# Decays of two heads at a time in a hybrid decoder layer: which PSUM banks they use and where they stand in the program

## The chip, the cores and the metric

The kernel runs on one core of one Trainium2 chip. The metric is the device time of one execution in microseconds (us): lower is better.

## What is computed

The reference is one decoder layer over 512 tokens of width 1024, in fp32: a SwiGLU feed-forward, two parallel token mixers (a gated delta rule of 8 heads, and a convolution module of width 31), a cross-attention into 256 memory tokens, and a second SwiGLU feed-forward, with a LayerNorm after each. The change touches one quantity of the delta rule, the decay of a head:

```python
gc = jnp.cumsum(g.reshape(b, n, CHUNK, h).transpose(0, 3, 1, 2), axis=-1)
diff = gc[..., :, None] - gc[..., None, :]
decay = jnp.where(tri, jnp.exp(jnp.where(tri, diff, 0.0)), 0.0)
m = jnp.where(strict, jnp.einsum("bhncd,bhnmd->bhncm", kb, kc) * decay, 0.0)
...
a_qk = jnp.einsum("bhncd,bhnmd->bhncm", qc, kc) * decay
```

So a head's decay is a matrix of exponentials per chunk that does not depend on q, k or v. It multiplies two products of the head: k with k (`m`) and q with k (`a_qk`). The kernel works with chunks of 128 tokens, four to a head.

## The kernel before

**Stages.** The program runs the first feed-forward, then the mixers, the cross-attention and the second feed-forward. All large products are done in three passes (`wh*xh`, `wl*xh`, `wh*xl`), each weight tile being split into a high and a low part: ScalarE casts the high part (L362) and VectorE subtracts (L110). One output tile of 128 channels by 512 tokens (`tile_job`, `a_tile`) is 24 products into one of four `acc` banks. `Weights.next` makes the tile in use and two more ahead of it; the high parts have four buffers (`WB = 4`).

**Mixers.** `mixers` first makes the tiles of the convolution's input gate (`glu`, a Sigmoid), five pairs of tiles, m = 0 to 4. Behind them come ten stages p = 0 to 9. Stage p < 8 makes the k, q and v tiles of head p; stages 0 and 1 also make the last three pairs of the gate (two in stage 0, so stage 0 has seven tiles: k, lin, gate, lin, gate, q, v). From stage 2 on a z tile is added. When a tile is finished, a chain of small steps for the head starts: `head_k` (short convolution on ScalarE and VectorE, Silu, transposes, norms, the product k with k, then the multiplication with the decay), an inversion (`invert_blocks` on GpSimd, `invert_rest` on TensorE), the scan over the chunks (`scan`), `head_q` (transposes, the product q with k, the decay) and `head_v`.

**What sets the order.** Within the stages TensorE's instructions are issued in the order in which the program writes them. An `Agenda` counts time by the columns that TensorE has been given (512 columns count 512/2400 us). Each step of a chain says after how many of these microseconds the next one is due (`PACE`), and between the k-steps of a tile (three products) the agenda runs every step that is due. So a step's TensorE instructions stand at a fixed place among the products of the tiles. If their operands are late, everything behind them on TensorE waits. Ahead of the stages there is no agenda. The order on ScalarE and VectorE is drawn up when the program is built, and each engine then takes its instructions in that order. Of the 31-tap convolution, VectorE gets a share between the steps (`taps`).

**PSUM.** There are four `acc` banks and four for the chains: `prep` has two, `inv` one, `scan` one (`BANKS`). `prep` is shared by the transposes of k, kb, q and v, the two products with the decay, and the decays; `inv` serves `invert_rest` and `scan` serves the scan, which also uses `acc` banks.

**A decay.** `decay` (L744) scales a triangle by the head's log-decays on ScalarE: eight instructions of 128x128 that make `ug` in two parts (`ug0`, `ug1`, one buffer each). Then it yields; in the agenda it goes on 6 us later. TensorE then makes three products of 128x512 into a `prep` bank, and ScalarE takes the exponential of the bank (L760) into `dd`. Heads 0 and 1 are done in the loop over m (at m = 3 and m = 4), heads 2 to 7 each at the start of the stage before their own (`if 2 <= p + 1 < HEADS`, L1177). Stage p's first microseconds are also when the q and v chains of head p - 1 come due. So TensorE takes the decay products of head p + 1 close to `head_v`'s transposes for head p - 1 (into the other `prep` bank) and to its product q with k, which needs a `prep` bank too.

ScalarE's Exp, Silu and Sigmoid each need another activation table: the rows call the switch ACT_TABLE_LOAD. Copy and Square are used between them without one.

Of the kernel before, what the change touches and what calls it, by code (L numbers as in the profile page):

```python
# [8 lines left out]
F32 = mybir.dt.float32  # L9
# [7 lines left out]
P = 128  # L17
# [17 lines left out]

TAPS = (5, 0.53, 4)
LAG = 3
PACE = dict(d=(6,), k=(6.6, 1.6, 4.6, 2.8), i=(37.5, 2, 3, 2, 2.3, 2, 2.5), b=(7.8, 1.25), s=(3.2, 2.1, 2.2, 1.8, 2.4, 2.1, 2.2, 1.5, 1.5, 3), q=(8, 5.5), v=(7.2,))
SLIP = 0
PAIRS = (2, 1)  # L40
GLU = 8 - sum(PAIRS)
# [257 lines left out]
class Kern:  # L299
# [441 lines left out]
        for j, t in enumerate((self.eg, self.edec, self.egl)):  # L741
            nc.scalar.activation(t.rearrange("p c h -> p (c h)"), cs[:, j * 32:(j + 1) * 32], AF.Exp)

    def decay(self, mp, h, dds):  # L744

        nc = self.nc
        ugs = []
        for i, g in enumerate((self.gh, self.gl)):
            ug = mp.tile([P, SEQ], F32R, name=self.nm("ug"), tag=f"ug{i}", bufs=1)
            for c in range(NCHK):  # L750
                nc.scalar.activation(ug[:, c * P:(c + 1) * P], self.con[:, K_U:K_U + P], AF.Copy,
                                     scale=g[:, c, h:h + 1].bitcast(F32))
            ugs.append(ug)
        yield
        ps = self.psum("prep")
        for i, ug in enumerate(ugs):
            self.mm(ps, lhsT=self.later, rhs=ug, start=(i == 0), stop=False)
        self.mm(ps, lhsT=self.idr, rhs=bc(self.never.unsqueeze(1), [P, NCHK, P]), start=False, stop=True)
        dd = mp.tile([P, SEQ], F32, name=self.nm("dd"), tag="dd", bufs=9)
        nc.scalar.activation(dd, ps, AF.Exp)  # L760
        dds[h] = dd

    def conv4(self, ps, dst, mt):

# [322 lines left out]
    def mixers(self, res, dst):  # L1087
        nc, tc = self.nc, self.tc
        S = 512
        with self.pages("mix") as (mp, self.small), ExitStack() as ctx:  # L1090
            ctx.enter_context(self.psum_pool("psm", **BANKS))
            self.small.tile([P, 8], F32, name="pad")
            cs, dds, self.convs, self.due = [], {}, [], 0

            def glu(pl, pg):
                m = len(cs)
                cs.append(self.glu(mp, m, pl, pg))
                self.convs.append(self.conv31(mp, m, cs[m]))
            ps = self.first
            for m in range(2):  # L1100
                glu(ps[2 * m], ps[2 * m + 1])
            self.gating(mp, self.a_tile())
            for m in range(2, GLU):
                lin = self.a_tile()
                self.taps(TAPS[0])
                glu(lin, self.a_tile())
                self.taps(TAPS[0])
                if m >= GLU - 2:
                    for _ in self.decay(mp, m - GLU + 2, dds):
                        pass  # L1110
            ozs = []
            with self.pages("heads") as (hp, self.small2):
                bufs = dict(kT=2, qT=3, ktok=3, MT=3, AT=3, vb=3, X=3, Y=3, tmp=4, z=3, bm=2, t1=2)

                def page(tag, dt=F32):
                    return hp.tile([P, S], dt, name=self.nm("pg"), tag=tag, bufs=bufs[tag])
                early = ["ktok", "X", "MT", "AT"] * 2
                late = ["bm", "t1", "ktok", "X", "MT", "AT", "bm", "t1"]
                hi_tags = ["kT"] * 2 + ["qT"] * 3 + ["z"] * 3
                lo_tags = ["vb"] * 3 + ["Y"] * 3 + ["tmp"] * 2  # L1120

                def pages(srcs):
                    hi, lo = [], []
                    for s, th, tl in zip(srcs, hi_tags, lo_tags):
                        hi.append(page(th, F32R))
                        lo.append(page(tl, F32R))
                        self.split(hi[-1], lo[-1], s)
                    return hi, lo

                def gate(tag):  # L1130
                    sg = page(tag)
                    nc.scalar.activation(sg, self.a_tile(), AF.Sigmoid)
                    return sg
                yp = []

                def tile_job(done):

                    ps = self.acc()
                    for k in self.a_steps(ps, self.W.next(), self.x_hi, self.x_lo, 0, SEQ):
                        if k == KT - 1:  # L1140
                            done(ps)
                        yield

                def gate_done(tag):
                    def done(ps):
                        yp.append(page(tag))
                        nc.scalar.activation(yp[-1], ps, AF.Sigmoid)
                    return done
                sts = [{} for _ in range(HEADS)]

                def on_k(h):
                    def chain(ps):
                        yield from paced(self.head_k(hp, h, ps, dds[h], sts[h]), PACE["k"])
                        yield from paced(self.invert_rest(hp, sts[h]), PACE["i"])
                        yield from paced(self.scan(mp, hp, h, sts[h], ozs), PACE["s"])
                    return lambda ps: agenda.start(chain(ps))

                def on_q(h):
                    return lambda ps: agenda.start(paced(self.head_q(hp, h, ps, sts[h]), PACE["q"]))

                def on_v(h):
                    return lambda ps: agenda.start(paced(self.head_v(hp, h, ps, sts[h]), PACE["v"]))
                self.bms = [page("bm"), page("bm")]
                for t in self.bms:
                    nc.gpsimd.memset(t, 0.0)
                self.agenda = agenda = Agenda()
                for p in range(HEADS + 2):
                    if p < HEADS:
                        jobs = [on_k(p), on_q(p), on_v(p)]
                    else:  # L1170
                        jobs = [gate_done(t) for t in early[4 * (p - HEADS):4 * (p - HEADS) + 4]]
                    for _ in range(PAIRS[p] if p < len(PAIRS) else 0):
                        lin = []
                        jobs[1:1] = [lin.append, lambda ps, lin=lin: glu(lin[0], ps)]
                    if p >= 2:
                        jobs.insert(0, lambda ps, p=p: self.head_z(hp, p - 2, ps, sts[p - 2]))
                    if 2 <= p + 1 < HEADS:  # L1177
                        agenda.start(paced(self.decay(mp, p + 1, dds), PACE["d"]))
                    for done in jobs:
                        for _ in tile_job(done):  # L1180
                            agenda.step()
                            self.taps(TAPS[1])
                agenda.finish()
                self.agenda = None
                oh, ol = pages(ozs)
                for m in range(8):
                    self.taps(TAPS[2])
                    ya = self.a_tile(lambda k, a, b: oh[k][:, a:b], lambda k, a, b: ol[k][:, a:b])
                    nc.vector.tensor_tensor(yp[m], yp[m], ya, op=ALU.mult)
                self.taps(8 * CW)  # L1190
                assert not self.convs
                sgc = []
                for t in range(NT):
                    for i, _ in enumerate(self.conv_norm(mp, cs, t)):
                        sgc.append(gate(late[2 * t]))
                    sgc.append(gate(late[2 * t + 1]))
                ch, cl = pages([c[:, 0:S] for c in cs])
                yh, yl = [], []
                for m in range(8):
                    yc = self.a_tile(lambda k, a, b: ch[k][:, a:b], lambda k, a, b: cl[k][:, a:b])  # L1200
                    nc.vector.scalar_tensor_tensor(sgc[m], yc, self.pcol(C_BCO + m), sgc[m], op0=ALU.add, op1=ALU.mult)
                    nc.vector.tensor_tensor(yp[m], yp[m], sgc[m], op=ALU.add)
                    h = mp.tile([P, S], F32R, name=self.nm("yh"), tag="dd", bufs=9)
                    l = mp.tile([P, S], F32R, name=self.nm("yl"), tag="c", bufs=8)
                    self.split(h, l, yp[m])
                    yh.append(h)
                    yl.append(l)
            ctx.close()
            with self.psum_pool("psl", gp=4), self.pages("ln2") as (lp, small):
                ln = LayerNorm(self, lp, small, 2, res, ALPHA, LN_EPS, dst, True)  # L1210
                self.b_form(KT, lambda k: yh[k], lambda k: yl[k], ln)
                self.first = ln.rest()
# [231 lines left out]
```

## Time and profile before

| what | value |
|---|---|
| median of 3 runs | 1533.62 us (1533.11 to 1535.7) |
| profiled execution, its own time | 1534.12 us |
| its span, first to last instruction | 1532.3 us |
| mean granted TensorE clock | 0.995 |
| TensorE busy | 1499.4 us, 98% of the span |
| VectorE, ScalarE, GpSimd busy | 961.4, 661.1, 156.9 us |

The span is that of the one profiled execution; 1.8 us of its own time lie outside the span. PE stands for TensorE's matmuls, PEld for its weight loads, DVE for VectorE, ACT for ScalarE, POOL for GpSimd. `L760` is line 760 of the kernel. A row such as `dd<-prep` is an instruction that reads tile `prep` and writes tile `dd`.

### The profile page before, as it was taken

How to read it: one execution, taken by the hardware profiler on the slowest of the kernel's cores; microseconds unless marked ns; L12 is line 12 of the kernel's file. 1: busy time of each engine (PE TensorE's matmuls, PEld its weight loads, DVE VectorE, ACT ScalarE, POOL GpSimd, SP SyncE). 2: the span in 40 equal slices, each digit the busy share in tenths (PEclk: the TensorE clock that was granted, in tenths of full speed). 3: DMA queues.
4: the chain of work that ended last, by engine and by line, in shares of the span. 5: the costliest groups of instructions: out<-in, count | busy, mean ns of one | idle time of the engine just before them, and what ended most of it. 6: DMA issues, size and time to landing. Idle time of an engine off the chain costs nothing.

```text
span 1532.3 us, 21736 instructions
## 1 busy us (share of the span) xinstructions
PE 1499.4 (98%) x8626; PEld 1296.3 (85%) x8626; DVE 961.4 (63%) x1356; ACT 661.1 (43%) x1236; POOL 156.9 (10%) x306
## 2 busy tenths in 40 slices
PE   7899999999999999999999999999999999999998
PEld 6899998889888777878888888899889888888886
DVE  7888875338879788778878355665756333333235
ACT  5455454232456766665553473134523222222110
POOL 0000000001004344444400000000000000000001
PEclk9999999999999999999999999999999999999999
DMA  7433325234132212222222223474324322222221
GB/s 274 177 111 111 111 70 178 97 110 165 56 102 90 90 61 70 78 79 78 89 101 83 83 74 118 167 255 149 119 85 163 138 97 96 96 97 96 96 97 55
DMA packets 65526, 170.97 MB, mean 112 GB/s; under 512 B 18768, under 2 KB 20944, under 8 KB 65360
## 3 DMA queue, kind: packets, MB, share of 16 engines
q1 hardware_dynamic: 65424, 169.57, 33.1%
q8 instruction: 68, 1.11, 0.3%
q14 instruction: 34, 0.28, 0.1%
HBM read 158.54 MB, written 12.06 MB: 111 GB/s over the span
## 4 chain that ended last, share of the span: by engine, by line
PE 83%; DVE 7%; issue 3%; POOL 3%; ACT 2%; DMA 2%; SPq 0%; DVEq 0%; POOLq 0%; ACTq 0%
PE acc L375 42%; PE acc L468 7%; PE gp L468 6%; PE acc L427 4%; PE acc L426 4%; PE acc L428 4%; PE gp L427 4%; PE gp L428 4%; PE gp L426 4%; PE inv L375 1%; DVE a L1042 1%; DVE wl L110 1%; POOL xt L778 1%; POOL xb L778 1%; DVE qT L110 1%
## 5 line engine op out<-in xcount | busy, mean ns | idle before, releaser
L110 DVE TENSOR_TENSOR wl<-w,wh 128x1024 fp32r<-128x1024 f32 (+1 forms) x220 | 265.3, 1209 | 309.5 <-ACT wh L362 308.4
L375 PE MATMUL acc<-xh,wh 128*128 128x512 f32 (+1 forms) x1032 | 396.7, 385 | 0.0
L375 PE MATMUL acc<-xl,wh 128*128 128x512 f32 (+1 forms) x1032 | 382.5, 371 | 0.1
L375 PE MATMUL acc<-xh,wl 128*128 128x512 f32 (+1 forms) x1032 | 382.0, 370 | 0.0
L362 ACT CAST wh<-w 128x1024 fp32r<-128x1024 f32 (+1 forms) x220 | 227.5, 1038 | 352.2 <-PE acc L375 135.4
L375 PEld LDWEIGHTS acc<-xl,wh 128*128 128x128 f32 x1032 | 194.4, 189 | 34.8 <-DVE xl L110 0.5
L375 PEld LDWEIGHTS acc<-xh,wh 128*128 128x128 f32 x1032 | 195.2, 189 | 28.7
L375 PEld LDWEIGHTS acc<-xh,wl 128*128 128x128 f32 x1032 | 195.4, 189 | 27.7
L1042 DVE SCALAR_TENSOR_TENSOR a<-c,par,a 128x512 f32<-128x512 f32 x232 | 174.8, 754 | 3.5
L261 POOL TENSOR_TENSOR mv<-mv,par 128x1 f32<-128x1 f32 x16 | 15.5, 971 | 986.0 <-DVE mv L260 986.0
L375 PE MATMUL acc<-pg,wh 128*128 128x512 f32 x256 | 79.8, 391 | 0.1
L375 PEld LDWEIGHTS acc<-pg,wh 128*128 128x128 f32 x256 | 48.0, 188 | 10.5 <-ACT pg L362 0.5
L468 PE MATMUL acc<-th,qh 128*128 128x256 f32 x176 | 50.9, 289 | 3.7 <-ACT qh L362 3.7
L468 PE MATMUL acc<-th,ql 128*128 128x256 f32 x176 | 51.0, 290 | 3.2 <-DVE ql L110 3.2
L682 DVE TENSOR_TENSOR s<-s,acc 128x512 f32<-128x512 f32 x22 | 15.1, 688 | 57.3 <-PE acc L375 57.2
L468 PE MATMUL acc<-tl,qh 128*128 128x256 f32 x176 | 50.6, 287 | 0.0
L375 PE MATMUL acc<-pg,wl 128*128 128x512 f32 x128 | 49.8, 391 | 0.0
L468 PE MATMUL gp<-th,qh 128*128 128x256 f32 x176 | 49.8, 283 | 0.0
L468 PE MATMUL gp<-th,ql 128*128 128x256 f32 x176 | 49.8, 283 | 0.0
L468 PE MATMUL gp<-tl,qh 128*128 128x256 f32 x176 | 49.8, 283 | 0.0
L681 ACT ACTIVATE s<-acc 128x512 f32<-128x512 f32 x22 | 13.1, 597 | 82.0 <-PE acc L375 82.0
L778 POOL TENSOR_TENSOR xb<-xb,xt 32x14 f32<-32x14 f32 (+6 forms) x112 | 47.5, 424 | 8.8
(377 smaller groups left out, 3135.8 us busy)
## 6 DMA issues: line engine op xcount, KB each, us to landing
w<-wall SPq DMA_DIRECT2D x216, 512.0 KB
res<-row SPq DMA_DIRECT2D x24, 256.0 KB
row<-res SPq DMA_DIRECT2D x12, 512.0 KB
wd<-wall SPq DMA_DIRECT2D x11, 512.0 KB
wc<-wall SPq DMA_DIRECT2D x11, 512.0 KB
wa<-wall SPq DMA_DIRECT2D x11, 512.0 KB
wb<-wall SPq DMA_DIRECT2D x11, 512.0 KB
lngb<-ln SPq DMA_DIRECT2D x8, 512.0 KB
```

The lines of the kernel that those rows point to most:

```text
L110: ins = getattr(self.kn.nc.vector, op)(*args, **kw)
L261: nc.gpsimd.tensor_tensor(mv[:, 3:4], mv[:, 2:3], self.kn.mh[:, 0:1], op=ALU.pow)
L362: self.nc.scalar.copy(hi, src)
L375: self.pin(self.nc.tensor.matmul(out, **kw), out.shape[-1] * (1 if kw["lhsT"].dtype == F32R else 4))
L426: mm(ps, lhsT=th, rhs=wh, start=first, stop=False)
L427: mm(ps, lhsT=th, rhs=wl, start=False, stop=False)
L428: mm(ps, lhsT=tl, rhs=wh, start=False, stop=last)
L468: self.tc.keep_in_program_order(self.nc.tensor.matmul(o, lhsT=a, rhs=b, start=(first and g == k == n == 0), stop=False, skip_group_check=T ...
L681: nc.scalar.activation(s, g, AF.Silu)
L682: nc.vector.tensor_tensor(s, s, u, op=ALU.mult)
L778: self.pool_pin(self.nc.gpsimd.tensor_tensor(out, x, y, op=op))
L1042: yield V.scalar_tensor_tensor(a, c[:, j:j + SEQ], w(j), a, op0=ALU.mult, op1=ALU.add)
```

## The change

`decay` becomes `decays` and takes two heads. For each of the two in turn it makes `ug`, yields, and issues the three products, the first head into the `inv` bank and the second into the `scan` bank. Behind both it issues the two exponentials one after the other. The pairs (0, 1) and (2, 3) are done in the loop over m, at m = 3 and m = 4; the pairs (4, 5) and (6, 7) are started in stage 0, at its first and at its fourth tile, with 6 us of agenda time ahead of each head's products. In the later stages there are no decays.

```diff
-PACE = dict(d=(6,), k=(6.6, 1.6, 4.6, 2.8), ...
+PACE = dict(d=(6, 6), k=(6.6, 1.6, 4.6, 2.8), ...
...
-    def decay(self, mp, h, dds):
+    def decays(self, mp, hs, dds):
 
         nc = self.nc
-        ugs = []
-        for i, g in enumerate((self.gh, self.gl)):
-            ug = mp.tile([P, SEQ], F32R, name=self.nm("ug"), tag=f"ug{i}", bufs=1)
-            for c in range(NCHK):
-                nc.scalar.activation(ug[:, c * P:(c + 1) * P], self.con[:, K_U:K_U + P], AF.Copy,
-                                     scale=g[:, c, h:h + 1].bitcast(F32))
-            ugs.append(ug)
-        yield
-        ps = self.psum("prep")
-        for i, ug in enumerate(ugs):
-            self.mm(ps, lhsT=self.later, rhs=ug, start=(i == 0), stop=False)
-        self.mm(ps, lhsT=self.idr, rhs=bc(self.never.unsqueeze(1), [P, NCHK, P]), start=False, stop=True)
-        dd = mp.tile([P, SEQ], F32, name=self.nm("dd"), tag="dd", bufs=9)
-        nc.scalar.activation(dd, ps, AF.Exp)
-        dds[h] = dd
+        banks = []
+        for h, tag in zip(hs, ("inv", "scan")):
+            ugs = []
+            for i, g in enumerate((self.gh, self.gl)):
+                ug = mp.tile([P, SEQ], F32R, name=self.nm("ug"), tag=f"ug{i}", bufs=1)
+                for c in range(NCHK):
+                    nc.scalar.activation(ug[:, c * P:(c + 1) * P], self.con[:, K_U:K_U + P], AF.Copy,
+                                         scale=g[:, c, h:h + 1].bitcast(F32))
+                ugs.append(ug)
+            yield
+            ps = self.psum(tag)
+            for i, ug in enumerate(ugs):
+                self.mm(ps, lhsT=self.later, rhs=ug, start=(i == 0), stop=False)
+            self.mm(ps, lhsT=self.idr, rhs=bc(self.never.unsqueeze(1), [P, NCHK, P]), start=False, stop=True)
+            banks.append(ps)
+        for h, ps in zip(hs, banks):
+            dds[h] = mp.tile([P, SEQ], F32, name=self.nm("dd"), tag="dd", bufs=9)
+            nc.scalar.activation(dds[h], ps, AF.Exp)
...
                 if m >= GLU - 2:
-                    for _ in self.decay(mp, m - GLU + 2, dds):
+                    for _ in self.decays(mp, (2 * (m - GLU + 2), 2 * (m - GLU + 2) + 1), dds):
                         pass
...
-                    if 2 <= p + 1 < HEADS:
-                        agenda.start(paced(self.decay(mp, p + 1, dds), PACE["d"]))
-                    for done in jobs:
+                    for i, done in enumerate(jobs):
+                        if p == 0 and i in (0, 3):
+                            hs = (4, 5) if i == 0 else (6, 7)
+                            agenda.start(paced(self.decays(mp, hs, dds), PACE["d"]))
                         for _ in tile_job(done):
                             agenda.step()
                             self.taps(TAPS[1])
```

## Rows read from the trace of the kernel before

**Rows 1.** The page: TensorE's busy time, and the chain that ended last.

```profile
PE 1499.4 (98%) x8626; PEld 1296.3 (85%) x8626; DVE 961.4 (63%) x1356; ACT 661.1 (43%) x1236; POOL 156.9 (10%) x306
...
PE 83%; DVE 7%; issue 3%; POOL 3%; ACT 2%; DMA 2%; SPq 0%; DVEq 0%; POOLq 0%; ACTq 0%
```

**Rows 2.** TensorE's waits from 400 to 800 us: total us, times, longest us.

```profile
PE prep L375 <- ACT dd L760: 5.4, 4, 2.3
PE prep L380 <- DVE AT L110: 0.8, 1, 0.8
PE prep L375 <- ACT vb L793: 0.7, 1, 0.7
```

**Rows 3.** Timeline, one of these waits, in stage 4: start, duration, instruction.

```profile
584.85 0.62 PE L375 MATMUL prep<-ug,later 128*128 128x512 f32 x2
...
585.54 0.60 PE L380 MATMUL prep<-con,vT 128*128 128x128 f32 x4
...
586.48 1.28 ACT L760 ACT_TABLE_LOAD   x1
587.78 0.60 ACT L760 ACTIVATE dd<-prep 128x512 f32<-128x512 f32 x1
...
588.43 1.75 PE L375 MATMUL prep<-qT,kT 128*128 128x128 f32 x8 [2.29 <-ACT dd L760]
```

**Rows 4.** Busy time by stretch around that wait; PEclk is the granted clock.

```profile
core 0: us, PE busy (x) PEld busy (x) DVE busy (x) ACT busy (x) POOL busy (x), PEclk, DMA share, GB/s
...
585.00:590.00 5.00, 2.71 (x17) 2.30 (x16) 2.35 (x4) 4.93 (x15) 0.00 (x0) 0.88 0.52 158
590.00:595.00 5.00, 5.00 (x24) 4.26 (x24) 2.12 (x4) 3.83 (x7) 2.02 (x2) 0.78 0.03 3
```

**Rows 5.** Busy time by stretch: stage 0 in two halves, then stages 1 to 6.

```profile
430.00:450.00 20.00, 20.00 (x92) 16.55 (x91) 14.86 (x23) 12.85 (x27) 2.19 (x4) 1.00 0.24 79
450.00:470.00 20.00, 20.00 (x96) 16.71 (x95) 19.54 (x25) 7.74 (x13) 5.39 (x11) 1.00 0.33 96
480.00:685.00 205.00, 196.24 (x1267) 161.67 (x1265) 163.61 (x258) 137.45 (x380) 82.50 (x166) 0.99 0.27 82
```

**Rows 6.** Timeline of TensorE in stage 7, which has no decay.

```profile
701.18 0.60 PE L380 MATMUL prep<-con,vT 128*128 128x128 f32 x4
701.62 1.06 PE L375 MATMUL prep<-qT,kT 128*128 128x128 f32 x8
```

**Rows 7.** Groups of ScalarE, 400 to 800 us: count, busy us, mean ns, idle before.

```profile
L751 ACT ACTIVATE ug<-con,gh 128x128 fp32r<-128x128 f32 x32 | 10.8, 402 | 0.0
L760 ACT ACT_TABLE_LOAD x8 | 10.3, 1283 | 0.1
...
L771 ACT ACT_TABLE_LOAD x5 | 6.4, 1283 | 8.3 <-DVE kT L110 4.5 <-DVE qT L110 3.8
L975 ACT ACT_TABLE_LOAD x5 | 6.4, 1283 | 0.1
```

**Rows 8.** Timeline of ScalarE around the start of stage 0.

```profile
421.98 1.27 ACT L751 ACTIVATE ug<-con,gh 128x128 fp32r<-128x128 f32 x4
423.16 1.27 ACT L751 ACTIVATE ug<-con,gl 128x128 fp32r<-128x128 f32 x4
...
432.60 1.04 ACT L362 CAST wh<-w 128x1024 fp32r<-128x1024 f32 x1
...
442.55 0.64 ACT L771 ACTIVATE kT<-kT 128x512 f32<-128x512 f32 x1
```

**Rows 9.** Timeline of TensorE around the start of stage 0.

```profile
430.44 0.39 PE L375 MATMUL prep<-never,idr 128*128 128x512 f32 x1
430.67 0.39 PE L375 MATMUL acc<-xh,wh 128*128 128x512 f32 x1
...
443.60 0.60 PE L380 MATMUL prep<-con,kT 128*128 128x128 f32 x4
```

More of the change, by code (lines that the diff above doesn't have):

```diff
@@ L37 @@
 LAG = 3
-PACE = dict(d=(6,), k=(6.6, 1.6, 4.6, 2.8), i=(37.5, 2, 3, 2, 2.3, 2, 2.5), b=(7.8, 1.25), s=(3.2, 2.1, 2.2, 1.8, 2.4, 2.1, 2.2, 1.5, 1.5, 3), q=(8, 5.5), v=(7.2,))
+PACE = dict(d=(6, 6), k=(6.6, 1.6, 4.6, 2.8), i=(37.5, 2, 3, 2, 2.3, 2, 2.5), b=(7.8, 1.25), s=(3.2, 2.1, 2.2, 1.8, 2.4, 2.1, 2.2, 1.5, 1.5, 3), q=(8, 5.5), v=(7.2,))
 SLIP = 0
```

## The prediction

> **What bounds the kernel now.** I read the page first. TensorE is busy for 98% of the span and carries 83% of the chain that ended last [rows 1]. So ScalarE time that the change saves is worth nothing by itself; only what TensorE waits for, and what its clock loses, can move the end. The change alters the stretch from 400 to 800 us, so I next asked for TensorE's waits there. The largest three are all for a `prep` bank that another engine still reads: 5.4 us in four waits for the decay's exponential, 0.8 us for `AT`, 0.7 us for `vb` [rows 2]. From 480 to 685 us, the stages with a decay, TensorE is idle for 205.00 - 196.24 = 8.8 us [rows 5]; 6.9 of them are these six waits.
>
> The timeline shows how one comes about [rows 3]. The decay's products start at 584.85 in one `prep` bank and the v transposes at 585.54 in the other. The product q with k is next and needs a bank. The exponential that frees the first bank stands behind an ACT_TABLE_LOAD of 1.28 us on ScalarE, starts at 587.78 and takes 0.60. TensorE goes on at 588.43, after 2.29 us. Then the granted clock is below full: 0.88 and 0.78 of it as means over two stretches of 5 us [rows 4], that is part of each at the lower level, 1.2 GHz. What TensorE did before was to stand idle for those 2.29 us.
>
> The trace holds its own control. At stage 7 there is no decay, and the same pair of instructions, v transposes at 701.18 and product q with k at 701.62, follows without a wait [rows 6].
>
> **The change part by part: the banks.** With `inv` and `scan` for the decays, and none in stages 1 to 6, the product q with k takes the `prep` bank that was freed before the v transposes, as in rows 6. The `AT` and `vb` waits have the same cause: a decay between two users of `prep` leaves them one bank to alternate in. So all six go. Their worth is at least the 6.9 us of idle time [rows 2]. It is a little more: a product is shown as 0.39 us long, while the next one starts 0.23 us after it (430.44 to 430.67 [rows 9]), so each wait hides another 0.16 us: 6.9 + 6 x 0.16 = 7.9 us. The upper bound is all idle time of the stretch, 8.8 us [rows 5]. I take 7.9. `inv` and `scan` are free at that time: their first users belong to head 0's inversion, which the agenda puts 37.5 us after `head_k`.
>
> **The clock.** (1 - 0.88) x 5 + (1 - 0.78) x 5 = 0.6 + 1.1 = 1.7 us of full-speed work [rows 4] come back, if no new wait of that length takes its place.
>
> **The exponentials side by side.** The eight loads in front of the decay's exponential become four; of the loads that restore Silu behind them (L771 and L975, five each [rows 7]) about six go with the decays of stages 1 to 6. That is ten times 1.28 us, 12.8 us of ScalarE. TensorE's chain does not hold them outside the waits already counted: no gain of their own. They can shorten the rest of the idle time, 8.8 - 6.9 = 1.9 us, or reordering can lengthen it; I take 0 with 1.9 either way.
>
> The Trainium skill, page "ScalarE: Activation LUTs", section "What ACT_TABLE_LOAD costs", puts a switch at about 1283 ns for the load and 1380 ns for a drain, 2.66 us in all. Rows 3 show the load at 1.28 us and the exponential 1.30 us after the load's start, so no drain of that length stands in the queue. By the Trainium skill's figure the four remaining pairs would each hold ScalarE 1.38 us longer; on the two loads near the critical place below that would be an estimated 2.8 us more of waiting and a sum of about 1528.8 us.
>
> **What is moved ahead.** The 24 decay products are all still made: nothing saved or added on TensorE. The `dd` tiles, nine buffers for eight decays and the outputs `oz`, suffice as before. No DMA is issued or moved. Weight casts run at least two tiles ahead of use; a tile is 24 products of 0.23, so they have 10.9 us, and ScalarE would have to be late by more than 9 before a tile waits for one.
>
> What can wait is a product with a fixed place. Scalings for one head take 424.43 - 421.98 = 2.45 us [rows 8], and `ug` has one buffer, so the next head's can begin only after the second product of the head before. At the start of stage 0 this becomes a chain. Head 2's products stand where head 1's did, until 430.7 [rows 9]. Head 3's scalings: to 433.1. Its products, three of 0.23: to 433.8. Load and two exponentials, 1.28 + 0.6 + 0.6: to 436.3. Head 4's scalings: to 438.8, or 439.8 with a cast of 1.04 [rows 8] between. Head 4's products are due 6 us of agenda after 430.67. The steps run every three products, so that is ten steps of 0.68, plus head 3's 0.7: 438.2. The wait is 0.6 to 1.6 us, and none where ScalarE takes the scalings ahead of the exponentials. Behind head 4's products in TensorE's queue stand the tiles of stage 0 and the transposes of head 0's k (443.60 [rows 9]), whose Silu ended at 442.55 + 0.64 = 443.19 [rows 8], only 0.4 us ahead; scalings of head 5 placed before it cost up to 2.45 us more, less what head 4's wait already gave. Head 1's and 3's products, ahead of the agenda, may each wait a few tenths. Together: 0 at the low end, 1.6 + 2.45 + 1 = 5 at the high end. I take 2.0, near the chain just worked out. Head 6's products wait for the `inv` bank, but are due some 16 us after head 4's, and the exponentials of heads 4 and 5 follow those by about 10: some 6 us of cover.
>
> **Sum.** -7.9 - 1.7 + 2.0 = -7.6 us. Against the profiled execution's 1534.12 that is 1526.5; the median of the runs lies 0.5 us lower, so 1526.0. With all bounds in its favour (-8.8 - 1.7 - 1.9) it is 1521.2; with the poor ones (-6.9 - 1.7 + 5) 1530.0.
>
> **The rivals.**
>
> *The waits move to stage 0.* ScalarE in 430 to 450 us is busy 12.85 of 20 us now [rows 5]. Out go the scalings that ran there for head 2 (2.45) and head 1's load and exponential (1.9); in come the scalings of heads 3, 4, 5 (7.4) and two pairs of exponentials (5.0): 20.9 of 20. Full, so the order decides. If head 4's products and head 0's transposes wait the 5 us above and the clock falls once (1.7), the sum is -7.9 - 1.7 + 5 + 1.7 = -2.9: 1530.7. Against it: 450 to 470 has room (7.74 + 7.4 of 20 us), and agenda steps shift together. Chance 0.17.
>
> *The time is given back.* TensorE runs sooner into VectorE, busy 163.61 of 205 us in these stages [rows 5], which then sets the pace in short stretches. If half of the 9.6 us returns: -4.8 + 2 = -2.8, 1530.8; all of it: +2, 1535.6. Against it: 41 us of VectorE idle time, and the missing wait of rows 6. Chance 0.10.
>
> *Slower: ScalarE becomes the bound of stage 0.* Three fixed places in the k chain of head 0 (head 4's products, the transposes, the product k with k) each wait for the full piece of ScalarE work ahead of them: 2.45 + 2.45 + 2.5 = 7.4, with a clock fall of 1.7 at each, 5.1: 12.5 against a gain of 8.6 (6.9 + 1.7): +3.9, 1537.5. It decides once those waits pass 8.6 us. For it speaks only the full 20 us of the first half. Chance 0.08.
>
> *It does not do what it says:* a Silu or Sigmoid falls between the two exponentials, and the loads stay. The banks still help: 1526 to 1529. Chance 0.03.
>
> **How the numbers follow.** My forecast has 0.62. The predicted time is 1526.0, with 1521.2 to 1530.0 as its own range. The range for 8 in 10 reaches up past the first rival and into the second: 1522 to 1533. About 0.2%, 3.1 us, is what a measurement can tell from no change, so faster means below 1530.5: all of the forecast, about half of the first rival, a third of the second, the last: 0.62 + 0.08 + 0.03 + 0.03 = 0.76. Same: 0.09 + 0.05 + 0.01 = 0.15. Slower: 0.09.
>
> **What would show it.** In the profile after: no wait of TensorE for `dd` on `prep`, and none of the 0.7 and 0.8; idle time in 480 to 685 under 3 us; a clock of 1.00 around 585 to 595; four loads at the exponential and about ten fewer in all. A new wait for `ug` on `inv` near 438 us would be the 2.0 us; one over 3 us, or a fall of the clock there, the first rival. I am wrong if TensorE's idle time in the stages stays near 9 us with `prep` free, or if weight tiles are late in stage 0.

## The result

The changed kernel takes 1526.24 us (median of 4 runs, 1526.11 to 1528.42) against 1534.43 us before: a ratio of 0.9949 with a 95% interval from 0.9937 to 0.9961, 8.2 us by the medians. In a second comparison on one chip (after_same, below) it was 1527.11 against 1534.17 us, a ratio of 0.995 (0.9937 to 0.9962). Forecast were 1526.0 us and a range from 1522 to 1533.

The page of the kernel after: busy time by engine, then the chain that ended last.

```profile
PE 1499.4 (98%) x8626; PEld 1297.2 (85%) x8626; DVE 961.9 (63%) x1356; ACT 651.1 (43%) x1228; POOL 161.7 (11%) x306
...
PE 89%; DVE 5%; ACT 2%; DMA 2%; POOL 1%; issue 1%; SPq 0%; DVEq 0%; POOLq 0%; ACTq 0%
```

TensorE does the same matmuls in the same busy time as in [rows 1], in a span of 1526.6 us. Its share of the chain rose from 83% to 89%. ScalarE has lost 10.0 us and eight instructions, all table loads.

TensorE's waits of the kernel after, 400 to 800 us (total us, times, longest us):

```profile
PE prep L380 <- DVE kb L110: 2.2, 3, 0.8
PE scan L375 <- ACT ug L753: 1.8, 2, 1.2
PE inv L375 <- ACT Y L924: 0.6, 1, 0.6
PE acc L375 <- DVE S L110: 0.2, 1, 0.2
```

All six waits of [rows 2] are gone. New are 1.8 us for `ug` and 0.6 for `Y`, and the waits for `kb` are three instead of one.

Busy time by stretch of the kernel after, columns as in [rows 4]: stage 0 in two halves, stages 1 to 6, and the place of the old clock fall.

```profile
430.00:450.00 20.00, 18.16 (x81) 14.48 (x80) 12.74 (x17) 17.67 (x43) 0.00 (x0) 1.00 0.24 85
450.00:470.00 20.00, 20.00 (x95) 16.38 (x94) 17.72 (x26) 16.33 (x35) 3.60 (x5) 1.00 0.29 94
480.00:685.00 205.00, 202.54 (x1321) 168.89 (x1320) 174.72 (x274) 117.93 (x350) 90.58 (x184) 1.00 0.27 84
585.00:590.00 5.00, 5.00 (x35) 4.49 (x34) 4.89 (x10) 3.55 (x14) 0.00 (x0) 1.00 0.47 161
```

TensorE's idle time in stages 1 to 6 fell from 8.8 us [rows 5] to 2.5, and the mean of its clock there is 1.00. ScalarE's table loads in these stages fell from 14 to 3; over 400 to 800 us they fell from 26 to 18. In stage 0 TensorE now idles 1.8 us of the first 20, where ScalarE is busy 17.67 instead of 12.85.

The new wait, timeline of TensorE in the kernel after:

```profile
432.28 0.39 PE L375 MATMUL inv<-never,idr 128*128 128x512 f32 x1
433.84 0.50 PE L375 MATMUL scan<-ug,later 128*128 128x512 f32 x1 [1.17 <-ACT ug L753]
435.01 0.50 PE L375 MATMUL scan<-ug,later 128*128 128x512 f32 x1 [0.67 <-ACT ug L753]
```

And ScalarE at the same time, and where it takes the exponentials of the pair (4, 5):

```profile
432.03 0.60 ACT L1034 ACTIVATE c<-acc 128x512 f32<-128x512 f32 x1 [1.13 <-PE acc L375]
432.52 1.27 ACT L753 ACTIVATE ug<-con,gh 128x128 fp32r<-128x128 f32 x4
433.69 1.27 ACT L753 ACTIVATE ug<-con,gl 128x128 fp32r<-128x128 f32 x4
434.98 1.28 ACT L764 ACT_TABLE_LOAD   x1
436.27 0.60 ACT L764 ACTIVATE dd<-inv 128x512 f32<-128x512 f32 x1
436.76 0.59 ACT L764 ACTIVATE dd<-scan 128x512 f32<-128x512 f32 x1
...
445.20 0.57 ACT L764 ACTIVATE dd<-inv 128x512 f32<-128x512 f32 x1
445.79 1.28 ACT L774 ACT_TABLE_LOAD   x1
447.09 0.64 ACT L774 ACTIVATE kT<-kT 128x512 f32<-128x512 f32 x1
...
450.90 1.28 ACT L764 ACT_TABLE_LOAD   x1
452.19 0.60 ACT L764 ACTIVATE dd<-scan 128x512 f32<-128x512 f32 x1
```

Head 2's products have just read `ug` when head 3's scalings start at 432.52. Both TensorE waits are for these. The pair (2, 3) shares one load (434.98), but the exponentials of heads 4 and 5 have a Silu with its load between them, so head 5's needs another.

### The profile page after: what moved, and what is told of

Its sections match the earlier page's. It is cut to its first block, busy times and chain, and to the rows that moved or that the text cites. A ratio compares the mean times of both kernels' runs of the same rounds, so it can differ in the third digit from the quotient of the medians.

```text
span 1526.6 us, 21727 instructions
## 1 busy us (share of the span) xinstructions
PE 1499.4 (98%) x8626; PEld 1297.2 (85%) x8626; DVE 961.9 (63%) x1356; ACT 651.1 (43%) x1228; POOL 161.7 (11%) x306
## 4 chain that ended last, share of the span: by engine, by line
PE 89%; DVE 5%; ACT 2%; DMA 2%; POOL 1%; issue 1%; SPq 0%; DVEq 0%; POOLq 0%; ACTq 0%
PE acc L375 47%; PE acc L468 7%; PE gp L468 5%; PE acc L427 4%; PE acc L426 4%; PE acc L428 4%; PE gp L428 4%; PE gp L427 4%; PE gp L426 4%; PE inv L375 2%; PE scan L375 1%; PE prep L375 1%; PE prep L380 1%; DVE wl L110 1%; PE gp L275 1%
## 5 line engine op out<-in xcount | busy, mean ns | idle before, releaser
L781 POOL TENSOR_TENSOR xt<-blk,xb 32x14 f32<-32x14 f32 (+6 forms) x112 | 49.0, 438 | 7.8
```

What stands on the lines that cost most here:

```text
L781: self.pool_pin(self.nc.gpsimd.tensor_tensor(out, x, y, op=op))
```

## The experiments

Three theories stood against each other. *Bank*, that of the prediction: TensorE no longer waits for a `prep` bank that a late exponential holds, and the clock does not fall. *Relief*: the gain is ScalarE's, which has fewer table loads to run in the stages. *Place or own banks*: it matters whether the pairs have banks of their own, or only that they are elsewhere. The first four kernels ran on one chip beside the kernel before at 1533.49 us.

**bank_only.** The kernel before, with another bank for the decay:

```diff
-        ps = self.psum("prep")
+        ps = self.acc()
         for i, ug in enumerate(ugs):
```

> The kernel before with one edit: a decay's products go into an acc bank instead of a prep bank. Its place, its single head and all its table loads stay. Theory bank (the gain is the prep bank that TensorE no longer waits for, 7.9 us, and the clock fall behind it, 1.7 us): about 1525 to 1527.5 us, no wait of TensorE on prep for dd, AT or vb, clock 1.00 around 585 to 595. Theory relief (the gain is ScalarE time, because fewer table loads run in the stages): 1533 us or more, since all loads are still there.

Measured: 1528.67 us, ratio 0.9964 (0.9951 to 0.9977). So 4.8 us, some 60 to 70% of what the change gives, with all 14 loads of stages 1 to 6 in their place; 1.2 us slower than the upper edge of what the bank theory gave, and far from the other's. Its largest waits of TensorE, 400 to 800 us:

```profile
PE scan L375 <- ACT vb L996: 1.7, 3, 1.0
PE inv L375 <- ACT t L890: 1.6, 2, 1.2
```

And its busy time in stages 1 to 6:

```profile
480.00:685.00 205.00, 200.28 (x1302) 165.75 (x1301) 168.62 (x265) 142.26 (x393) 86.69 (x172) 1.00 0.27 82
```

The `prep` waits for `dd`, `AT` and `vb` are gone and the clock holds, but 4.7 us of idle time remain there. The rows hold 3.3 us of waits for other tiles of ScalarE; 0.8 us of these, 0.4 for each tile, stood in the kernel before too, so 2.5 are new. Its timeline shows what is in front of the longest of them:

```profile
584.50 1.28 ACT L760 ACT_TABLE_LOAD   x1
585.79 0.60 ACT L760 ACTIVATE dd<-acc 128x512 f32<-128x512 f32 x1
586.28 1.13 ACT L793 ACTIVATE vb<-prep,beta 128x128 f32<-128x128 f32 x4
587.44 1.28 ACT L975 ACT_TABLE_LOAD   x1
588.73 0.60 ACT L975 ACTIVATE z<-acc 128x512 f32<-128x512 f32 x1
...
589.51 0.58 ACT L890 COPY t<-inv 128x512 f32<-128x512 f32 x1
```

On TensorE, the products that the copy reads and those that wait for it:

```profile
586.51 1.05 PE L375 MATMUL inv<-X,pg 128*128 128x128 f32 x8
...
590.14 0.60 PE L375 MATMUL inv<-t,Y 128*128 128x128 f32 x3 [1.20 <-ACT t L890]
```

The copy of `t` is due about 587.6, when the products into `inv` that started at 586.51 are done; it comes at 589.51, behind the load that brings Silu back and the Silu itself, and TensorE waits for it until 590.14.

**no_load.** The kernel before, without the exponential of heads 2 to 7, and so without their decay:

```diff
-        nc.scalar.activation(dd, ps, AF.Exp)
+        if h < 2:
+            nc.scalar.activation(dd, ps, AF.Exp)
+        else:
+            nc.scalar.activation(dd, ps, AF.Copy, scale=0.0)
```

> The kernel before, with the exponential of heads 2 to 7 replaced by a Copy with scale 0 of the same size: it leaves out the decay of these heads, and with it the table loads in front of and behind it; bank and place stay. Theory bank: the bank is held 1.28 us less each time, so the four dd waits shrink from 5.4 to under 1.5 us, the AT and vb waits of 0.8 and 0.7 may stay, and the clock does not fall: 1527.5 to 1529.5 us. Theory relief: as much as the change or more, 1524 to 1526.5 us, since all twelve loads of the stages are gone.

Measured: 1527.82 us, ratio 0.9959 (0.9945 to 0.9973), inside the bank theory's span and 1.3 us over the other's. Stages 1 to 6 hold 2 table loads instead of 14, and the clock holds. What remains on `prep`, beside 0.8 us for `kb`:

```profile
PE prep L375 <- ACT dd L763: 0.9, 1, 0.9
...
PE prep L375 <- ACT vb L796: 0.7, 1, 0.7
```

So the shared bank is cheap, 1.6 us against 6.9, when no load makes its reader late.

**bank_no_load.** Both edits in one, run later beside a kernel before at 1534.64 us; it leaves out the decay of heads 2 to 7.

> bank_only and no_load in one: the kernel before with the decay's products in an acc bank, and the exponential of heads 2 to 7 replaced by a Copy with scale 0 (it leaves out the decay of these heads and the table loads around it). The place stays. If the three microseconds of other waits in bank_only come from the loads, and the 1.6 us of prep waits in no_load from the bank, both are gone and the time is that of the changed kernel without its ug wait: 1524 to 1526.5 us, TensorE's waits from 400 to 800 us under 2 us. If the place has a worth of its own (decay work on ScalarE in the stages), it stays at 1527.5 us or more.

Measured: 1525.45 us, ratio 0.994 (0.9925 to 0.9955). No `prep` wait but one of 0.8 us for `kb`, 2.8 us of waits in all from 400 to 800 us, a little over what was expected, and idle time of 205.00 - 202.47 = 2.5 us in stages 1 to 6, as in the changed kernel:

```profile
480.00:685.00 205.00, 202.47 (x1317) 168.23 (x1316) 171.81 (x271) 126.53 (x382) 87.11 (x173) 1.00 0.28 86
```

That is 9.2 us off with the decay still in its old place. Without the shared bank and without the loads, moving it shows no further worth.

**moved_prep.** The changed kernel with `prep` for both heads of a pair:

```diff
-        for h, tag in zip(hs, ("inv", "scan")):
+        for h, tag in zip(hs, ("prep", "prep")):
```

> The changed kernel with both heads of a pair in the two prep banks instead of inv and scan. Theory bank: stages 1 to 6 are as in the changed kernel, but in stage 0 the first head's bank is held until both exponentials, so the transposes of head 0's k and kb wait there: 2 to 5 us in stage 0, 1528 to 1531.5 us. If banks of their own do nothing and only the place counts: 1526 us, as the changed kernel.

Measured: 1527.35 us, ratio 0.9959 (0.9944 to 0.9974), not told apart from the changed kernel. The 2 to 5 us did not come: the waits are the same 1.8 us for `ug`, 1.6 for `kb`, 0.6 for `Y` as in after_same, and none in stage 0 for a bank. My expectation was wrong here. TensorE's decay products of heads 4 and 5, and head 0's k transposes between them:

```profile
441.73 0.61 PE L375 MATMUL prep<-ug,later 128*128 128x512 f32 x2
...
447.86 0.60 PE L380 MATMUL prep<-con,kT 128*128 128x128 f32 x4
...
448.99 0.62 PE L375 MATMUL prep<-ug,later 128*128 128x512 f32 x2
```

ScalarE takes head 4's exponential at 444.52, before head 5's products have started, as with the pair (4, 5) above. So no bank is held when the transposes and head 5's products come. Once the decays have left stages 1 to 6, banks of their own add nothing that can be told from noise.

**loads_back.** The changed kernel with a tiny exponential from a constant in each of stages 1 to 6.

```diff
+    def loads(self):
+        yield
+        t = self.small.tile([P, 8], F32, name=self.nm("ld"), tag="ld", bufs=2)
+        self.nc.scalar.activation(t, self.pcol(C_ALOG, 8), AF.Exp)
...
+                    if 2 <= p + 1 < HEADS:
+                        agenda.start(paced(self.loads(), (6,)))
```

> The changed kernel with a tiny exponential (128x8, from a constant) put into each of stages 1 to 6 where the decay was: no bank, no TensorE work, but two table loads per stage, 15 us of ScalarE time in all. Theory bank: 1526 to 1528 us, at most a few tenths per stage where a load falls in front of something TensorE waits for. Theory relief: 1531 us or more.

Measured: 1527.92 us, ratio 0.9966 (0.9953 to 0.9979). It tells nothing: the exponential waits for no data of its stage, and all six ran from 393.9 to 394.4 us, far ahead of the stages. Stages 1 to 6 hold 3 loads, and ScalarE is busy there for 118.4 us, as in the changed kernel (117.9). Hence the next one.

**loads_tied.** The changed kernel with a tiny exponential that reads `head_q`'s sums of squares:

```diff
         self.sumsq(hp, sq, tq)
+        if h < 6:
+            ld = self.small2.tile([P, NCHK], F32, name=self.nm("ld"), tag="ld", bufs=2)
+            nc.scalar.activation(ld, sq, AF.Exp, scale=0.0)
```

> The changed kernel with a tiny exponential of 128x4 behind head_q's sums of squares for heads 0 to 5, which it reads, so that it can't be drawn ahead as in loads_back: two table loads in each of stages 1 to 6, without a bank and without TensorE work. Theory bank: 0 to 2 us over the changed kernel beside it. Theory relief: 4 us or more over it. Middle ground, since in bank_only TensorE waited 3 us for other tiles behind the loads: 2 to 4 us over it, from waits for vb and t on ScalarE.

Measured: 1537.3 us (1534.24 to 1539.61 in 11 runs), ratio 1.0014 (1.0005 to 1.0023) to the kernel before, and 10.2 us over the changed kernel on the same chip (after_same). This is far beyond the bank theory's 2 us and the middle ground's 4; only the other theory's "4 us or more" holds it. Its new waits of TensorE, 400 to 800 us:

```profile
PE acc L375 <- ACT vb L1002: 2.7, 2, 2.5
...
PE inv L375 <- ACT t L796: 1.7, 1, 1.7
...
PE prep L380 <- ACT vT L774: 1.2, 2, 0.9
PE prep L380 <- ACT kT L774: 1.0, 1, 1.0
```

And its busy time in stages 1 to 6:

```profile
480.00:685.00 205.00, 195.54 (x1252) 162.11 (x1252) 166.73 (x261) 127.62 (x349) 81.68 (x167) 0.98 0.27 84
```

In front of the longest wait, until 666.58 us, ScalarE has:

```profile
662.66 1.28 ACT L960 ACT_TABLE_LOAD   x1
...
663.96 0.20 ACT L960 ACTIVATE ld<-ssq 128x4 f32<-128x4 f32 x1
664.18 1.28 ACT L774 ACT_TABLE_LOAD   x1
```

Silu of `vT` follows at 665.47, and only then the `vb` that TensorE waits for, at 666.16.

TensorE idles 9.5 us in stages 1 to 6 instead of 2.5. Its clock falls twice, to a mean of 0.91 from 520 to 540 us and of 0.93 from 660 to 685: (1 - 0.91) x 20 + (1 - 0.93) x 25 = 3.6 us of full-speed work. None of the waits is for a bank that a decay holds, since no decay is left in these stages. The twelve loads, 15.4 us of ScalarE, stand in another place than those before did, in front of the v chain. bank_only has about as many loads in these stages, 14 against 15, and its new waits are 2.5 us, so the price goes by the place. A part of it is not the loads': VectorE overwrites the sums that the added exponential reads, and waited for it three times, 0.8 us in all. But that loads in the stages cost only through the shared bank is refuted.

**after_same, ug_own and exp_single** ran beside loads_tied, with the kernel before at 1534.17 us. The first is the changed kernel again.

> The changed kernel again, for a comparison on one chip with the three beside it: 1526 to 1528 us, with its one new wait, TensorE for head 3's ug, at 1.8 us of idle time.

Measured: 1527.11 us, with 1.8 us of waits for `ug`. ug_own gives heads 1 and 3 a `ug` in buffers that are free then:

```diff
-                ug = mp.tile([P, SEQ], F32R, name=self.nm("ug"), tag=f"ug{i}", bufs=1)
+                own = h in (1, 3)
+                ug = mp.tile([P, SEQ], F32R, name=self.nm("ug"), tag="dd" if own else f"ug{i}", bufs=9 if own else 1)
```

> The changed kernel with buffers of their own (free dd buffers) for the ug of heads 1 and 3, so that their scalings need not wait until the products of heads 0 and 2 have read the single ug buffers. If the new wait in front of stage 0 is the single buffer: both ug waits of 1.17 and 0.67 us gone, 2.3 us faster than the changed kernel beside it. If it is ScalarE's load (its order, with the gate's Sigmoid and the table loads ahead), the wait stays at over 1 us and the time is that of the changed kernel.

Measured: 1524.19 us (1523.29 to 1524.73), ratio 0.9931 (0.9918 to 0.9943), 2.9 us faster than the changed kernel beside it and the fastest of all that compute the whole layer. The `ug` waits, 1.8 us of idle time, are gone. Its timeline of TensorE:

```profile
431.33 0.62 PE L375 MATMUL inv<-ug,later 128*128 128x512 f32 x2
431.79 0.39 PE L375 MATMUL inv<-never,idr 128*128 128x512 f32 x1
432.01 0.62 PE L375 MATMUL scan<-ug,later 128*128 128x512 f32 x2
```

Head 3's products now follow head 2's at once; its scalings run from 425.46 on, straight behind head 2's. The single buffer was the wait.

exp_single puts each exponential behind its own products:

```diff
-        banks = []
...
             self.mm(ps, lhsT=self.idr, rhs=bc(self.never.unsqueeze(1), [P, NCHK, P]), start=False, stop=True)
-            banks.append(ps)
-        for h, ps in zip(hs, banks):
             dds[h] = mp.tile([P, SEQ], F32, name=self.nm("dd"), tag="dd", bufs=9)
             nc.scalar.activation(dds[h], ps, AF.Exp)
```

> The changed kernel with each head's exponential right behind its own products instead of two side by side: banks and places as in the changed kernel. Theory bank: the same within 1 us, with up to eight loads at the exponential instead of five. Theory relief: 1 to 4 us over the changed kernel beside it, since stage 0's ScalarE is full and gets up to 5 us of loads more.

Measured: 1530.0 us, ratio 0.9972 (0.9962 to 0.9982), 2.9 us over the changed kernel. That is outside the bank theory's 1 us. It is inside the other's 1 to 4, but not for its reason: there are no more table loads from 400 to 800 us than in the changed kernel, 18 each. TensorE's waits differ from the changed kernel's in one. Its timeline on both engines:

```profile
431.43 1.28 ACT L761 ACT_TABLE_LOAD   x1
432.73 0.60 ACT L761 ACTIVATE dd<-inv 128x512 f32<-128x512 f32 x1
433.22 1.27 ACT L752 ACTIVATE ug<-con,gh 128x128 fp32r<-128x128 f32 x4
...
434.54 0.50 PE L375 MATMUL scan<-ug,later 128*128 128x512 f32 x1 [3.08 <-ACT ug L752]
```

And its busy time by stretch:

```profile
430.00:450.00 20.00, 16.25 (x58) 12.63 (x57) 11.88 (x16) 14.29 (x34) 0.00 (x0) 0.83 0.19 55
```

Head 2's exponential with its load now stands ahead of head 3's scalings on ScalarE. TensorE waits 3.08 us instead of 1.17, and its clock falls: (1 - 0.83) x 20 = 3.4 us of full-speed work in this execution. With the 1.9 us of longer waiting that is 5.3, more than the 2.9 by the medians; exp_single_ug, with the same wait, has a mean clock of 0.91 there, 1.8 us, so the price of the fall is not the same each time.

**exp_single_ug.** exp_single with the buffers of ug_own, beside the kernel before at 1534.64 us.

> exp_single with the ug buffers of ug_own: each head's exponential right behind its own products, but heads 1 and 3 have ug buffers of their own. If exponentials side by side are worth only that no exponential with its load gets between the products of head 2 and the scalings of head 3 on ScalarE, the wait of 3.1 us and the clock fall behind it are gone and the time is that of ug_own, 1523.5 to 1525.5 us. If the order of the exponentials costs in another way too, it stays 1.5 us or more above ug_own.

Measured: 1530.51 us, ratio 0.9972 (0.9962 to 0.9982), as exp_single and not as ug_own. I expected the wait to go; it stays at 3.1 us, with the same load, exponential and scalings in front of it. ScalarE starts these scalings at 435.19, right behind the exponential and with no idle time between: what holds them is not the buffer but their place in the order drawn up for ScalarE, behind the exponential that is written before them. So the order of writing is what side by side is worth here, and the buffer helps only with it.

**ug_own_pace.** ug_own with `k=(6.6, 1.6, 5.9, 2.8)`, beside the same kernel before.

> ug_own with the third pace of the k chain at 5.9 instead of 4.6, so that the transposes of kb come two k-steps later. If the two waits for kb of 0.8 us are a place two steps too early, they go and the time falls by 1 to 2 us, to 1522 to 1523.5 us. If the rest of the chain comes late behind it (the chain is 1.4 us longer per head), the time stays within 0.7 us of ug_own or rises.

Measured: 1525.7 us, ratio 0.9942 (0.993 to 0.9955). The `kb` waits go, but 1.2 us for `MT` and 1.5 for `vb` come, and by the ratios the time is no better than ug_own's. The gap moves along the chain.

## Why the prediction was right

*The six waits and the clock.* Right in what happens: none of the six is left and the clock holds. Their term, 7.9 us, is 6.3 in idle time (8.8 to 2.5 us), or somewhat more with what each wait hides: 6.9 went and 0.6 came back in small waits. The clock is 1.00 where it had lost 1.7 us, as forecast.

*Why they go.* Here the reasoning was too narrow. I put the gain on the bank and wrote that the chain does not hold the loads outside the waits already counted. bank_only frees the bank and gets 4.8 us; no_load takes the loads away and gets 5.7; both together get 9.2. Most of the waiting needed both a shared bank and a reader that a load made late. With the bank freed alone, the loads that stay in the stages let TensorE wait 2.5 us more for `vb` and `t`, and bank_no_load, without the loads, is rid of these; loads_tied shows that twelve loads in another place can cost 10.2 us without any shared bank. So the step "no gain of their own" is the one that failed, and the forecast held because moving the decays takes the bank's user and its loads away at once. The Trainium skill, page "ScalarE: Activation LUTs", section "Table sets: the hidden batching unit", advises to batch activations by table set. The Trainium skill's advice agrees with these traces as far as bank_no_load (2 loads in stages 1 to 6, 1525.45 us, against 14 and 1528.67 in bank_only) and loads_tied (15 loads, 10.2 us over the changed kernel) go. In exp_single the number of loads from 400 to 800 us, 18, did not change, and its 2.9 us come from their order.

*Loads.* I forecast ten fewer and four at the exponential. There are eight fewer and five: two of the four pairs are not side by side. The rival in which a Silu or a Sigmoid falls between two exponentials came true for these pairs, at no visible cost: from 430 to 480 us, where they stand, TensorE waits for nothing but head 3's `ug`.

*The new wait.* The term of 2.0 us is 1.8 in idle time, and ug_own, without it, is 2.9 us faster. What makes it was right: the single `ug` buffer, scalings of 2.45 us, ScalarE's order. Its place was wrong. By the prediction's own figures head 3's scalings end at 433.1 and head 2's products at 430.7, so head 3's products had to wait some 2.4 us; I had allowed a few tenths there and counted head 4's 6 us of agenda from 430.67, as if head 3's products did not stand between. Head 4's products come at 442.41 instead of 438.2, 2.7 us behind their scalings, and do not wait. That 2.0 and 1.8 are close is luck.

*Banks of their own.* Right that they are free, but without effect at this place, by moved_prep.

*The rivals.* The first, waits that move to stage 0, happened to 1.8 us and without a clock fall; exp_single shows how near it was: one exponential in another order brings 3.1 us and the fall. ScalarE in 430 to 450 us is busy 17.67 us, short of the 20.9 worked out. The second, time given back, happened in small: in stages 1 to 6 the waits for `kb`, which VectorE writes, rose from 0.6 to 1.6 us and one of 0.6 for `Y` came, while 1.1 us of other small waits went. No weight tile came late.

*The sum.* -7.6 us forecast, -8.2 and -7.1 us by the medians of the two comparisons. The bounds of the forecast's own range were added up wrongly: 1521.2 takes off 8.8 and 1.9, although the 1.9 is a part of the 8.8, and 1530.0 leaves the 1.9 out. By the same terms they are 1523.1 and 1531.9; the measured time lies inside either pair.

## What to carry to other kernels

Here a PSUM bank that rotated among several users was as slow as its latest reader: before adding a user, look at what stands in front of its reader on the reading engine, a table load above all. Taking out either the sharing or the lateness gave more than half of the gain. Such edits must not be added up: alone they took 4.0 and 5.0 us off TensorE's idle time in stages 1 to 6, together 6.2, and either alone brought the clock back. When work is moved ahead, its own single buffers become the next wait: giving `ug` a second home was worth another 2.9 us here, 1.8 of them as waits, and the order in which the next head's inputs and the last head's outputs are written decided whether that could help.

## What the runs showed of the hardware

A table load took 1.28 us in every run; what it cost went by what stood behind it on ScalarE. Twelve of them cost 10.2 us in loads_tied, in a kernel whose ScalarE is busy 43% of the time, while the loads of the pairs in stage 0 of the changed kernel made TensorE wait for nothing.

The granted clock fell after TensorE had been idle for 1.66 us (loads_tied, until 523.87: a mean of 0.69 from 525 to 530 us), 2.29 us (the kernel before, [rows 4]), 2.47 us (loads_tied, until 666.58: 0.80 from 665 to 670 us) and 3.08 us (exp_single: 0.51 from 435 to 440 us). It stayed at 1.00 after 1.32 and 1.54 us of idling in the kernel before (until 517.95 and 665.78).

The clock also differs where the kernels do not. In the first feed-forward, which no edit touches, its mean from 20 to 70 us is 0.93 in the profiles of the kernel before, bank_no_load, loads_tied, ug_own and exp_single, and 0.90 in all others, both profiles of the changed kernel among them:

```profile
20.00:70.00 50.00, 43.81 (x325) 42.92 (x326) 44.06 (x46) 23.59 (x31) 0.00 (x0) 0.90 0.52 197
```

That is (0.93 - 0.90) x 50 = 1.5 us between profiled executions that no edit explains by what it changes. It makes the profile of the changed kernel look worse beside that of the kernel before, and ug_own's 2.9 us and bank_no_load's 9.2 may hold as much of it. Which of the two the other executions had is not shown. Differences of one or two microseconds were therefore read from repeated runs and from the waits, not from two spans.
